# Choosing the 256 best keys by interpolated thresholds, with the small updates on GpSimd and the adaLN sums on VectorE

## The chip, the cores and the metric

The kernel runs on one core of a Trainium2 chip. The metric is the device time of one execution in microseconds. Three runs of the kernel before gave 1230.46, 1232.58 and 1237.68 us, so the median is 1232.58 us.

## The reference

Two decoder layers run one after the other on a sequence of 1024 positions with 1024 features in float32. In each layer:

```
mod = silu(c) @ w_ada + b_ada            # shift, scale, gate: adaLN
h = layer_norm(x) * (1 + scale) + shift
proj = h @ w_in                          # u, v, z_a | q, k, val, z_b | q_idx, k_idx, w_idx
y_a = silu(z_a) * spatial_gating_unit(u, v, ...)         # chunks of 128
score[t, s] = sum_h w_idx[t, h] * relu(q_idx[t, h] . k_idx[s] / 8)   # s <= t only
idx = top_k(score, 256)                  # per row t, 256 keys
y_b = silu(z_b) * softmax(q . k[idx]) @ val[idx]         # 8 heads
x = layer_norm(ALPHA * x + gate * (concat(y_a, y_b) @ w_out))
```

For the work at hand the middle lines matter: every row t has scores for its t + 1 earlier positions, and attention may use only the 256 largest. Rows 0 to 255 have at most 256 keys, so a selection is needed for the six blocks 2 to 7 of 128 rows each, with 384, 512, ..., 1024 columns.

## The kernel before

Rows lie on the 128 partitions. Products with `w_in` and `w_out` are made from high and low float32r halves, three matmuls for each tile of 128 by 512 (L326, L735). A layer goes through these stages:

- The keys, values and half of the indexer queries are projected (`kv`, `queries`). Then `scores` (L496) makes the six score tiles `sc2` to `sc7`: TensorE (L506), a ReLU on ScalarE (L508) and an accumulation on VectorE (L513).
- The remaining projections follow: `v_path`, `queries`, `u_za` and `zb`, one weight pair after the other. The weights are split in two halves by ScalarE and GpSimd (L279, L280). The spatial gating `sgu` (L445) lies between them. Each projection yields after a tile, and after each yield `side()` (L905) takes steps of generators that are not part of the projections. Those are the searches for the thresholds, and, in the second half of the stage, the adaLN sums (`ada_sum`, L166).
- The masks are finished by `select_mask` (L636), `w_out` is loaded and scaled with the adaLN gate (`load_wout`, L710, with products on VectorE and GpSimd at L717 and L720), and the attention runs over the blocks in the order `ORDERS[l]`: 1, 0, 2, 3, ... in the first layer, 4, 5, 6, 2, 3, 7, 1, 0 in the second.

A framework below the kernel gives out buffers and semaphores and settles the order of the instructions on each engine in advance, from a simulated timeline; on the chip each engine then works through its own list in order. All loads go through the one queue of SyncE.

The selection before the change looks for the exact 256th largest score by its bits, one bit per step, and has three forms. Blocks 7, 6 and 5 (`select` with `on_act`, L527) take 31 steps with a sign-and-sum on ScalarE for each block (L544) and two operations on one column on VectorE (L545, L553). Blocks 4 and 3 (`select16`, L590) are searched in two passes of 16 steps over 16-bit keys, with a count (L574) and two operations on one column (L583, L585) for each block. Block 2 takes 31 steps with a count at L519 and L552, L553. `select_mask` then counts twice (L642, L644), numbers the equal scores by a running sum (L647), and makes the mask of 0 and -3e38 with two passes on VectorE (L648, L649) and one on GpSimd (L650).

An adaLN sum adds up eight products of a 128 by 1024 weight tile with one column of the condition. On GpSimd that is a product (L182) and a sum (L184) for each tile. The first layer makes three such sums (its gate and the next layer's shift and scale), 24 tiles; the second layer makes one, 8 tiles. The buffer of a tile is free again for the next load (L163, on the SyncE queue) when its product has been added.

Of the kernel before, what the change touches and what calls it, by code (L numbers as in the profile page):

```python
# [22 lines left out]
S = 1024  # L23
# [4 lines left out]
TOP = 256  # L28
EPS = 1e-5
# [19 lines left out]

class Trunk:  # L50
    BUFS = dict(h=16, ya=4, wr=2, w=6, r=6, kd=2, vv=1, q=2, ga=6, gb=3, gc=4)
    PBUFS = dict(acc=2, s=2, pt=3, o=1)
    GROUPS = ((0, 7, 6, 5), (16, 4, 3), (32, 2))
    MLEAD = 16
# [9 lines left out]
    ADAE = (0, 0, 0)  # L64
# [30 lines left out]
    def consts(self):  # L95
# [9 lines left out]
        nc.gpsimd.memset(self.mhalf, -0.5)  # L105
        self.ones = self.col("ones", 1)
# [389 lines left out]
    def scores(self, l, i):  # L496
        nc = self.nc
        n = (i + 1) * P
        q = self.load_q(l, 1, i)
        sc = self.t(f"sc{i}", [P, n])  # L500
        for h in range(8):
            for c0, w in self.chunks(i):
                self.scn += 1
                pl = self.p(self.SC_PS[self.scn % len(self.SC_PS)])
                for x in range(2):
                    nc.tensor.matmul(pl[:, :w], q[:, h, :], self.KI[x][:, c0:c0 + w], start=(x == 0), stop=(x == 1))  # L506
                r = self.g(self.SC_R[self.scn % len(self.SC_R)])
# [12 lines left out]

    def int_tile(self):
        return self.col("bi", 14, 4, I32)

    def cnt_tile(self):
        return self.col("cnt", 12, 4)

    def select(self, scs, blocks, on_act):  # L527
        nc, G = self.nc, len(blocks)
        ns = [(i + 1) * P for i in blocks]
        cnt = self.cnt_tile()  # L530
        for c in range(G):
            self.count(scs[c], ns[c], 0.0, ALU.is_ge, cnt[:, c:c + 1])
        m = self.int_tile()
        nc.vector.tensor_scalar(m[:, :G], cnt[:, :G], float(TOP), -1.0, op0=ALU.is_lt, op1=ALU.mult)
        f = self.int_tile()
        nc.vector.tensor_scalar(f[:, :G], m[:, :G], 1 << 30, -(1 << 31) if on_act else 0, op0=ALU.bitwise_xor, op1=ALU.bitwise_xor)
        yield
        for b in range(30, -1, -1):
            cnt, dec = self.cnt_tile(), self.int_tile()
            for c in range(G):  # L540
                thr = f[:, c:c + 1].bitcast(F32)
                if on_act:
                    j = self.t("junka", [P, S], I8)
                    nc.scalar.activation(j[:, :ns[c]], scs[c], AF.Sign, bias=thr, accum_out=cnt[:, c:c + 1])  # L544
                    nc.vector.tensor_scalar(dec[:, c:c + 1], cnt[:, c:c + 1], float(2 * TOP - 1 - ns[c]), float(1 << b),  # L545
                                            op0=ALU.is_lt, op1=ALU.mult)
                else:
                    self.count(scs[c], ns[c], thr, ALU.is_ge, cnt[:, c:c + 1])
            f2 = self.int_tile()
            for c in range(G):  # L550
                if not on_act:
                    nc.vector.tensor_scalar(dec[:, c:c + 1], cnt[:, c:c + 1], float(TOP), float(1 << b), op0=ALU.is_lt, op1=ALU.mult)  # L552
                nc.vector.tensor_scalar(f2[:, c:c + 1], dec[:, c:c + 1], f[:, c:c + 1], (1 << b) >> 1,  # L553
                                        op0=ALU.bitwise_xor, op1=ALU.bitwise_xor)
            f = f2
            yield
        if on_act:
            mag, g, up = self.int_tile(), self.int_tile(), self.cnt_tile()
            nc.vector.tensor_scalar(mag[:, :G], f[:, :G], 0x7FFFFFFF, None, op0=ALU.bitwise_and)
            nc.vector.tensor_scalar(up[:, :G], mag[:, :G].bitcast(F32), 1.25 * 2.0 ** -24, 2.0 ** -149, op0=ALU.mult, op1=ALU.max)  # L560
            nc.vector.tensor_tensor(g[:, :G].bitcast(F32), up[:, :G], f[:, :G].bitcast(F32), op=ALU.subtract)
            nc.vector.tensor_scalar(f[:, :G], f[:, :G], -(1 << 31), None, op0=ALU.bitwise_xor)
            cnt, ok = self.cnt_tile(), self.int_tile()
            for c in range(G):
                self.count(scs[c], ns[c], g[:, c:c + 1].bitcast(F32), ALU.is_ge, cnt[:, c:c + 1])
            nc.vector.tensor_scalar(ok[:, :G], cnt[:, :G], float(TOP), None, op0=ALU.is_ge)
            nc.vector.copy_predicated(f[:, :G], ok[:, :G], g[:, :G])
        for c, i in enumerate(blocks):
            self.thr[i] = f[:, c:c + 1].bitcast(F32)
        yield  # L570

    def count16(self, keys, thr, out):
        j = self.t("junkd", [P, 6 * P], BF16)
        self.nc.vector.tensor_scalar(j[:, :keys.shape[1]], keys, thr, None, op0=ALU.is_ge, op1=ALU.add, accum_out=out)  # L574

    def search16(self, keys, t):
        nc, G = self.nc, len(keys)
        for b in range(15, -1, -1):
            cnt, dec, t2 = (self.cnt_tile() for _ in range(3))
            for c in range(G):  # L580
                self.count16(keys[c], t[:, c:c + 1], cnt[:, c:c + 1])
            for c in range(G):
                nc.vector.tensor_scalar(dec[:, c:c + 1], cnt[:, c:c + 1], float(TOP), -float(1 << b), op0=ALU.is_lt, op1=ALU.mult)  # L583
            for c in range(G):
                nc.vector.tensor_scalar(t2[:, c:c + 1], dec[:, c:c + 1], t[:, c:c + 1], float((1 << b) >> 1), op0=ALU.add, op1=ALU.add)  # L585
            t = t2
            yield
        return t

    def select16(self, scs, blocks):  # L590
        nc, G = self.nc, len(blocks)
        store, off, keys = self.u("r", (P, 2 * S), I16), 0, []
        for c, i in enumerate(blocks):
            n = (i + 1) * P
            k = store[:, off:off + n]
            off += n
            hi = scs[c].bitcast(I16).rearrange("p (n two) -> p n two", two=2)[:, :, 1]
            nc.vector.tensor_scalar(k, hi, 0.0, 32767.0, op0=ALU.is_lt, op1=ALU.mult)
            nc.vector.tensor_tensor(k, k, hi, op=ALU.bitwise_xor)
            keys.append(k)  # L600
        t = self.cnt_tile()
        nc.vector.memset(t[:, :G], 0.0)
        yield
        t = yield from self.search16(keys, t)
        neg = self.cnt_tile()
        sg, of = self.cnt_tile(), self.cnt_tile()
        nc.vector.tensor_scalar(neg[:, :G], t[:, :G], 0.0, None, op0=ALU.is_lt)
        nc.vector.tensor_scalar(sg[:, :G], neg[:, :G], -2.0, 1.0, op0=ALU.mult, op1=ALU.add)
        nc.vector.tensor_scalar(of[:, :G], neg[:, :G], 65535.0, None, op0=ALU.mult)
        low = []  # L610
        for c, i in enumerate(blocks):
            n = (i + 1) * P
            lw = self.g("gb", (P, 2 * HALF), U16)[:, :n]
            src = scs[c].bitcast(U16).rearrange("p (n two) -> p n two", two=2)[:, :, 0]
            nc.vector.tensor_scalar(lw, src, sg[:, c:c + 1], of[:, c:c + 1], op0=ALU.mult, op1=ALU.add)
            nc.vector.scalar_tensor_tensor(lw, keys[c], t[:, c:c + 1], lw, op0=ALU.is_equal, op1=ALU.mult)
            k = keys[c].bitcast(U16)
            nc.vector.tensor_scalar(k, keys[c], t[:, c:c + 1], 65535.0, op0=ALU.is_gt, op1=ALU.mult)
            nc.vector.tensor_tensor(k, k, lw, op=ALU.max)
            low.append(k)  # L620
        u = self.cnt_tile()
        nc.vector.memset(u[:, :G], 32768.0)
        yield
        u = yield from self.search16(low, u)
        f, m = self.int_tile(), self.int_tile()
        nc.vector.tensor_copy(f[:, :G], t[:, :G])
        nc.vector.tensor_copy(m[:, :G], u[:, :G])
        f2, m2, f3 = self.int_tile(), self.int_tile(), self.int_tile()
# [431 lines left out]
```

## Time and profile before

| | |
|---|---|
| median of 3 runs | 1232.58 us |
| the profiled execution, its own time | 1233.29 us |
| its span, first to last instruction | 1231.5 us |
| TensorE / VectorE busy | 1119.0 us / 977.5 us |
| ScalarE / GpSimd busy | 707.1 us / 706.5 us |
| mean granted TensorE clock | 0.963 of full speed |

The shares are means over stages that differ. In time, with us from the start of the span: first the adaLN of layer 0 and its first projections to about 110, scores to about 205, projections with the searches to about 410, attention of layer 0 to about 700, scores of layer 1 to about 812, projections with the searches to about 1007, attention to the end. A matmul's busy time includes time in which it waits in the pipeline, so a busy TensorE is not one at its peak.

### The profile page before, as it was taken

The page shows a single profiled execution, that of the slowest core. Times are in us where ns is not written, and L with a number is a line of the kernel's source. Part 1 is how long each engine was busy: PE and PEld are TensorE (multiplying, and loading weights), DVE is VectorE, ACT ScalarE, POOL GpSimd, SP SyncE. Part 2 cuts the span into 40 slices and gives each one's busy share as a digit, 9 for nine tenths or more (in the row PEclk, how much of TensorE's full clock was granted, in tenths as well). Part 3 has the DMA queues.
Part 4 walks back from the last instruction along what each step waited for, and adds up shares of the span by engine and source line. Part 5 has one row for each costly group of instructions (what it writes and reads, how often), then busy time and mean ns, then how long its engine had stood idle before and what let it go on. Part 6 is the DMA issues. An engine that isn't in the chain of part 4 may idle for free.

```text
span 1231.5 us, 18024 instructions
## 1 busy us (share of the span) xinstructions
PE 1119.0 (91%) x5456; PEld 887.3 (72%) x5456; DVE 977.5 (79%) x2776; ACT 707.1 (57%) x1344; POOL 706.5 (57%) x556
## 2 busy tenths in 40 slices
PE   5989999897999499989989999999899967999997
PEld 1568888766788388766667788877678856777885
DVE  6784767998989965788976467599999898878775
ACT  0342655778794164565765345557789535667561
POOL 1574314997794785564765531189633378555753
PEclk9899999998999799999999999999999988999999
DMA  8936332347454474331322463144431434333311
GB/s 257 275 104 165 104 86 79 136 138 222 140 170 154 142 222 125 103 112 44 94 86 69 120 172 86 52 163 137 147 125 52 141 100 142 83 104 86 112 35 60
DMA packets 126777, 152.15 MB, mean 124 GB/s; under 512 B 17108, under 2 KB 94292, under 8 KB 126680
## 3 DMA queue, kind: packets, MB, share of 16 engines
q1 hardware_dynamic: 126680, 151.01, 40.3%
q8 instruction: 43, 0.70, 0.2%
q14 instruction: 54, 0.44, 0.1%
HBM read 111.38 MB, written 35.40 MB: 119 GB/s over the span
## 4 chain that ended last, share of the span: by engine, by line
PE 49%; DVE 30%; issue 7%; ACT 6%; DMA 6%; SPq 2%; POOL 0%; DVEq 0%; ACTq 0%; POOLq 0%
PE pacc L326 18%; PE pacc L735 13%; DVE junkd L574 4%; PE ps L673 4%; PE ppt L693 4%; DVE junkd L519 3%; PE ppt L506 3%; ACT junka L544 3%; PE po L699 2%; PE po L698 2%; PE ps L506 2%; DMA h<-in_w_ada 1%; DVE gb L647 1%; DVE bn L211 1%; DVE bi L553 1%
## 5 line engine op out<-in xcount | busy, mean ns | idle before, releaser
L326 PE MATMUL pacc<-h,w 128*128 128x512 f32 (+2 forms) x2304 | 550.0, 393 | 13.0 <-ACT gc L472 4.8
L326 PEld LDWEIGHTS pacc<-h,w 128*128 128x128 f32 (+1 forms) x2304 | 423.6, 189 | 111.2 <-ACT gc L472 6.4
L280 POOL TENSOR_TENSOR w<-wr,w 128x512 fp32r<-128x512 f32 (+1 forms) x100 | 131.6, 1334 | 168.4 <-ACT w L279 161.2
L544 ACT ACTIVATE junka<-sc,bi 128x1024 int8<-128x1024 f32 x186 | 193.5, 1040 | 51.0 <-DVE bi L553 23.4
L735 PE MATMUL pacc<-h,gc 128*128 128x512 f32 x768 | 196.5, 400 | 2.9 <-ACT gc L279 2.5
L735 PEld LDWEIGHTS pacc<-h,gc 128*128 128x128 f32 x768 | 142.6, 191 | 31.8 <-ACT gc L279 3.2
L513 DVE SCALAR_TENSOR_TENSOR sc<-gc,wi,sc 128x384 f32<-128x384 f32 (+3 forms) x140 | 101.8, 768 | 52.6 <-ACT gc L508 50.1
L673 PE MATMUL ps<-kd,q 128*128 128x512 f32 (+4 forms) x384 | 106.2, 376 | 31.5 <-DVE mx L674 24.8
L697 DVE TENSOR_TENSOR ga<-ppt,ga 128x512 fp32r<-128x512 f32 x144 | 96.6, 684 | 18.1 <-ACT ga L696 17.2
L696 ACT ACTIVATE ga<-ppt 128x512 fp32r<-128x512 f32 x144 | 82.7, 593 | 34.8 <-PE ppt L693 33.6
L574 DVE TENSOR_SCALAR_CACHE_REDUCE junkd<-r,cnt 128x640 bf16<-128x640 int16 (+3 forms) x128 | 102.5, 801 | 0.1
L673 PEld LDWEIGHTS ps<-kd,q 128*128 128x128 f32 x384 | 65.6, 198 | 49.5 <-DVE mx L674 37.1
L682 POOL TENSOR_SCALAR w<-w,rd 128x256 f32<-128x256 f32 (+6 forms) x77 | 62.5, 815 | 42.5 <-DVE rd L681 22.7
L679 ACT ACTIVATE w<-w,mx 128x256 f32<-128x256 f32 (+6 forms) x77 | 60.7, 788 | 42.6 <-DVE mx L674 42.0
L279 ACT ACTIVATE w<-wr 128x512 fp32r<-128x512 f32 (+1 forms) x100 | 56.0, 598 | 44.1 <-DMA wr<-in_w_in 22.0
L693 PE MATMUL ppt<-ident,w 128*128 128x128 f32 x349 | 75.5, 277 | 0.3 <-ACT gc L256 0.3
L216 POOL TENSOR_TENSOR rs<-rs,mhalf 128x1 f32<-128x1 f32 x48 | 32.1, 676 | 73.1 <-DVE rs L215 73.0
L693 PE MATMUL ppt<-ident,ya 128*128 128x128 f32 x227 | 59.1, 277 | 15.4 <-DVE modT L192 15.4
L698 PE MATMUL po<-ga,vv 128*128 128x512 f32 x144 | 62.1, 431 | 9.4 <-DVE gb L705 6.4
L508 ACT ACTIVATE gc<-ppt 128x384 f32<-128x384 f32 (+3 forms) x96 | 47.9, 525 | 36.9 <-PE ppt L506 31.5
L184 POOL TENSOR_TENSOR r<-r,r 128x1024 f32<-128x1024 f32 x28 | 68.2, 2437 | 0.1
L345 POOL TENSOR_TENSOR ga<-ga,ga 128x512 fp32r<-128x512 f32 (+2 forms) x40 | 48.4, 1215 | 33.5 <-ACT ga L344 29.2
(202 smaller groups left out, 2109.4 us busy)
## 6 DMA issues: line engine op xcount, KB each, us to landing
wr<-in_w_in SPq DMA_DIRECT2D x50, 512.0 KB, 4.2
r<-in_w_ada SPq DMA_DIRECT2D x32, 512.0 KB, 4.3
q<-q SPq DMA_DIRECT2D x112, 128.0 KB, 3.0
q<-ga SPq DMA_DIRECT2D x48, 256.0 KB, 2.2
h<-in_w_ada SPq DMA_DIRECT2D x32, 256.0 KB, 5.4
wr<-in_w_out SPq DMA_DIRECT2D x16, 512.0 KB, 4.0
r<-r SPq DMA_DIRECT2D x14, 512.0 KB, 3.4
r<-x SPq DMA_DIRECT2D x12, 512.0 KB, 4.2
```

The lines of the kernel that those rows point to most:

```text
L184: eng.tensor_tensor(acc, acc, w, op=ALU.add)
L280: self.nc.gpsimd.tensor_tensor(lo, src, hi.bitcast(F32), op=ALU.subtract)
L326: self.nc.tensor.matmul(acc[:m, :tn], w[:, k, :m], h[:, k % 2, t0:t0 + tn], start=(k == 0 and i == 0), stop=(k == NK - 1 and i == 2))
L513: nc.vector.scalar_tensor_tensor(sc[:, c0:c0 + w], r[:, :w], wsc, sc[:, c0:c0 + w], op0=ALU.mult, op1=ALU.add)
L544: nc.scalar.activation(j[:, :ns[c]], scs[c], AF.Sign, bias=thr, accum_out=cnt[:, c:c + 1])
L574: self.nc.vector.tensor_scalar(j[:, :keys.shape[1]], keys, thr, None, op0=ALU.is_ge, op1=ALU.add, accum_out=out)
L673: nc.tensor.matmul(ps[:, :w], q[:, g * 4 + h, :], self.KD[x][:, c0:c0 + w], start=(x == 0), stop=(x == 1))
L693: nc.tensor.transpose(pt[:, h * P:(h + 1) * P], pr[h][:, kt * P:(kt + 1) * P], self.ident)
L696: nc.scalar.activation(ph, pt, AF.Copy)
L697: nc.vector.tensor_tensor(pl, pt, ph.bitcast(F32), op=ALU.subtract)
L698: nc.tensor.matmul(o, self.V[:, kt, :], ph, start=(kt == 0), stop=False)
L735: self.nc.tensor.matmul(acc, s[:, k, :], m[:, cs], start=(first and k == i == 0), stop=(not more and k == 3 and i == 2))
```

## The change

All three searches are replaced by one, in two groups: blocks 2, 3, 4 and blocks 5, 6, 7. From the mean and the deviation of the first 256 scores of each row, and from a table that is loaded once (`ztab`), it makes a first threshold and a bracket around it. Then there are six steps. In each, VectorE counts the scores at or above the threshold for the three blocks, and GpSimd narrows the bracket and interpolates the next threshold, all three blocks in one instruction of a few columns. A row has what it needs when the upper end of its bracket counts 248 to 255 scores. The number of rows for which that isn't so is summed by TensorE and read into a register of VectorE. If it isn't 0, a branch runs `exact`, the old bit search, for the three blocks of the group. The masks are made within the same generator: the scores at or above the threshold are set aside by two passes, the up to eight that are still missing are found with `max` (eight largest of a row) and marked with `match_replace`, and a last pass turns the marks into 0 and -3e38. `side()` now takes one step of one group in turn instead of one step of each search. The adaLN sums within the layers run on VectorE, where each tile is one instruction, a product and a sum together (L174, L176).

```
-    GROUPS = ((0, 7, 6, 5), (16, 4, 3), (32, 2))
-    MLEAD = 16
+    GROUPS = ((2, 3, 4), (5, 6, 7))
+    STEPS = 6
-    ADAE = (0, 0, 0)
+    ADAE = (1, 1, 1)
...
     def rope_tables(self):
+        nc.sync.dma_start(self.ztab, a["ztab"][:, 0:36].rearrange("p (k g) -> p k g", k=6))
+        nc.sync.dma_start(self.iota8, a["ztab"][:, 36:44])
...
+    def select(self, masks, blocks, grp):
...
+        for c, i in enumerate(blocks):
+            nc.vector.bn_stats(st[:, 0, :], masks[i][:, 0:256])
+            nc.vector.bn_aggr(mv[:, c, :], st[:, 0:1, :])
...                                  # 9 GpSimd instructions: first threshold V, bracket Z
+        yield
+        for k in range(self.STEPS):
+            for c, i in enumerate(blocks):
+                self.count(masks[i], (i + 1) * P, V[:, 0, c:c + 1], ALU.is_ge, C[:, c:c + 1])
+            pool.tensor_scalar(V[:, 1, :], C, 1.0, -float(MID), op0=ALU.mult, op1=ALU.add)
+            pool.tensor_scalar(M[:, 0, :, :], rep(C, 2), float(TOP), 1.0, op0=ALU.is_lt, op1=ALU.mult)
+            pool.tensor_scalar(M[:, 1, :, :], rep(C, 2), float(TOP), 1.0, op0=ALU.is_ge, op1=ALU.mult)
+            pool.tensor_scalar(M[:, 2, :, :], rep(C, 2), float(TOP), 1.0, op0=ALU.is_lt, op1=ALU.mult)
+            pool.tensor_tensor(pair(Z), pair(Z), M[:, 0:2].rearrange(...), op=ALU.mult)
+            pool.tensor_tensor(pair(U), cols(V)..., M[:, 1:3].rearrange(...), op=ALU.mult)
+            pool.tensor_tensor(Z, Z, U, op=ALU.add)
...                                  # k == 0: 5 more, the first step; k == 5: none
+            elif k + 1 < self.STEPS:
+                pool.tensor_tensor(W[:, 0, :], Z[:, 0, :], Z[:, 2, :], op=ALU.subtract)
+                pool.tensor_scalar(R, Z[:, 3, :], -0.5, 1.0, op0=ALU.min, op1=ALU.mult)
+                pool.tensor_tensor(W[:, 1, :], Z[:, 1, :], R, op=ALU.subtract)
+                pool.tensor_tensor(R, W[:, 1, :], self.minus6[:, :G], op=ALU.pow)
+                pool.tensor_tensor(R, R, W[:, 0, :], op=ALU.mult)
+                pool.tensor_tensor(R, R, Z[:, 1, :], op=ALU.mult)
+                pool.tensor_tensor(V[:, 0, :], Z[:, 0, :], R, op=ALU.subtract)
+            yield
+        pool.tensor_scalar(bad, Z[:, 3, :], float(TOP - 8 - MID), 1.0, op0=ALU.is_lt, op1=ALU.mult)
+        for c in range(G):
+            nc.tensor.matmul(pt[0:1, 0:1], bad[:, c:c + 1], self.ones[:, 0:1], ...)
+        nc.vector.tensor_copy(flag, pt[0:1, 0:1])
+        v = nc.vector.value_load(flag[0:1, 0:1])
+        with self.tc.If(v != 0):
+            for c, i in enumerate(blocks):
+                self.exact(masks[i], (i + 1) * P)       # bit search: 33 counts, then 7 passes
+                nc.vector.memset(Z[:, 2, c:c + 1], 1.5)
+                nc.vector.memset(Z[:, 3, c:c + 1], float(TOP - 8 - MID))
...                                  # 5 GpSimd instructions: Q, how many are missing
+        for c, i in enumerate(blocks):
+            nc.vector.tensor_scalar(w[:, :n], sc, Z[:, 2, c:c + 1], -2.0 * LOW, op0=ALU.is_lt, op1=ALU.mult)
+            nc.vector.scalar_tensor_tensor(sc, w[:, :n], LOW, sc, op0=ALU.add, op1=ALU.min)
+            yield
+            nc.vector.max(m8, sc)
+            nc.vector.tensor_tensor(m8, m8, Q[:, c, :], op=ALU.min)
+            yield
+            nc.vector.match_replace(sc, m8, sc, LOW)
+            nc.vector.tensor_scalar(sc, sc, LOW, NEG, op0=ALU.not_equal, op1=ALU.mult)
+            yield
-    def select_mask(self, sc, i):
...
             while owed >= 1:
                 owed -= 1
-                for g in gens:
-                    next(g, None)
+                while gens and next(gens[0], 0) == 0:
+                    gens.pop(0)
+                gens.append(gens.pop(0)) if gens else None
```

## Rows read from the trace of the kernel before

**Rows 1.** The page's first part: busy time of each engine

```profile
PE 1119.0 (91%) x5456; PEld 887.3 (72%) x5456; DVE 977.5 (79%) x2776; ACT 707.1 (57%) x1344; POOL 706.5 (57%) x556
```

**Rows 2.** Windows: stretch, length; busy PE, PEld, DVE, ACT, POOL; PEclk, DMA, GB/s

```profile
205.00:435.00 230.00, 196.95 (x966) 158.00 (x965) 214.61 (x776) 151.08 (x273) 185.74 (x126) 0.93 0.51 161
812.00:1050.00 238.00, 210.02 (x1013) 166.80 (x1011) 224.44 (x811) 161.16 (x284) 150.40 (x102) 0.94 0.40 129
...
410.00:435.00 25.00, 8.14 (x43) 6.55 (x42) 22.55 (x34) 8.54 (x18) 18.27 (x9) 0.59 0.46 152
...
990.00:1050.00 60.00, 41.34 (x184) 32.94 (x182) 55.38 (x99) 26.11 (x42) 49.25 (x26) 0.83 0.41 137
...
435.00:700.00 265.00, 244.98 (x1230) 193.00 (x1231) 191.35 (x486) 150.56 (x296) 167.28 (x148) 0.98 0.36 107
```

**Rows 3.** Waits of PE, 205 to 435 and 812 to 1050: us, times, longest

```profile
PE ppt L693 <- DVE modT L192: 15.4, 1, 15.4
...
PE ps L673 <- DVE mx L674: 15.3, 5, 9.3
```

**Rows 4.** Groups of VectorE instructions, 205 to 435: sum us, mean ns, idle before

```profile
L574 DVE TENSOR_SCALAR_CACHE_REDUCE junkd<-r,cnt 128x640 bf16<-128x640 int16 (+1 forms) x64 | 51.2, 801 | 0.0
...
L553 DVE TENSOR_SCALAR bi<-bi,bi 128x1 int32<-128x1 int32 x124 | 23.2, 204 | 0.4
...
L647 DVE TENSOR_TENSOR_SCAN gb<-gb 128x384 f16<-128x384 f16 (+5 forms) x6 | 9.7, 1622 | 0.0
L649 DVE SCALAR_TENSOR_TENSOR sc<-sc,bi,gb 128x384 f32<-128x384 f32 (+5 forms) x6 | 9.4, 1559 | 0.0
L457 DVE SCALAR_TENSOR_TENSOR ya<-po,vg,bsum 128x128 f32<-128x128 f32 x32 | 9.2, 334 | 0.0
...
L644 DVE TENSOR_SCALAR_CACHE_REDUCE gb<-sc,bi 128x384 f16<-128x384 f32 (+5 forms) x6 | 5.6, 930 | 0.0
...
L514 DVE TENSOR_TENSOR sc<-sc,mask 128x128 f32<-128x128 f32 x1 | 0.3, 279 | 0.0
...
L622 DVE MEMSET cnt<- 128x2 f32 x1 | 0.1, 60 | 0.0
```

**Rows 5.** Groups of VectorE by shape, whole run, like passes elsewhere

```profile
L855 DVE SCALAR_TENSOR_TENSOR ga<-h,cond,ga 128x512 f32<-128x512 f32 x14 | 12.2, 874 | 0.1
...
L720 DVE TENSOR_TENSOR h<-wr,h 128x1024 fp32r<-128x1024 f32 x4 | 5.6, 1412 | 0.2 <-ACT h L719 0.2
...
L220 DVE TENSOR_SCALAR q<-q,mv,rs 128x1024 f32<-128x1024 f32 x6 | 4.8, 808 | 1.4 <-POOL rs L216 1.4
```

**Rows 6.** Groups of GpSimd, 205 to 435

```profile
L184 POOL TENSOR_TENSOR r<-r,r 128x1024 f32<-128x1024 f32 x21 | 51.0, 2430 | 0.1
...
L182 POOL TENSOR_SCALAR r<-r,cond 128x1024 f32<-128x1024 f32 x24 | 30.1, 1257 | 26.0 <-PE ps L506 17.4 <-DMA r<-in_w_ada 8.6
...
L650 POOL TENSOR_SCALAR sc<-sc 128x384 f32<-128x384 f32 (+5 forms) x6 | 9.8, 1628 | 15.8 <-DVE bi L630 11.8 <-DVE sc L649 4.0
```

**Rows 7.** GpSimd by shape, whole run: the smallest ones, and L682 at two sizes

```profile
L216 POOL TENSOR_TENSOR rs<-rs,mhalf 128x1 f32<-128x1 f32 x48 | 32.1, 676 | 73.1 <-DVE rs L215 73.0
...
L682 POOL TENSOR_SCALAR w<-w,rd 128x1024 f32<-128x1024 f32 x10 | 11.6, 1155 | 1.6 <-DVE rd L681 1.2 <-DVE nmb L229 0.3
...
L682 POOL TENSOR_SCALAR w<-w,rd 128x256 f32<-128x256 f32 x19 | 10.1, 539 | 3.9 <-DVE rd L681 3.9
...
L107 POOL MEMSET ones<- 128x1 f32 x1 | 0.1, 99 | 0.0
```

**Rows 8.** ScalarE, whole run: the sign-and-sum of the old search

```profile
L544 ACT ACTIVATE junka<-sc,bi 128x1024 int8<-128x1024 f32 x186 | 193.5, 1040 | 51.0 <-DVE bi L553 23.4 <-DVE bi L545 13.7 <-DVE bi L536 6.6
```

**Rows 9.** SyncE queue: a wait in all, an issue (start, us); a load (KB, us to landing)

```profile
SPq L163 <- POOL r L184: 42.4, 17, 5.3
...
7.15 0.43 SPq L126 DMA_DIRECT2D invf<-in_inv_freq  x1
...
r<-cs_tab SPq DMA_DIRECT2D x16, 128.0 KB, 7.2
```

More of the change, by code (lines that the diff above doesn't have):

```diff
@@ L22 @@
 D = 1024
-S = 1024
+S = SEQ = 1024
 DEPTH = 2
@@ L28 @@
 TOP = 256
+MID = 252
+LOW = -2.0 ** 126
 EPS = 1e-5
@@ L47, in two_pi_parts, with start_table @@
     return parts
+def start_table():
+    import numpy as np
+    from statistics import NormalDist
+    nd = NormalDist()
+    tab = np.zeros((P, 6, 6), np.float32)
+    for i in range(2, NB):
+        for p in range(P):
+            n = i * P + p + 1
+            z = nd.inv_cdf(1.0 - (MID + 0.5) / (n + 1))
+            above = lambda y: n * (1.0 - nd.cdf(y)) - MID
+            tab[p, :, i - 2] = (z - 2.0, z, z + 2.0, min(above(z + 2.0), -9.0), above(z - 2.0), 1.0 / (n * nd.pdf(z)))
+    return np.concatenate([tab.reshape(P, 36), np.tile(np.arange(8, dtype=np.float32), (P, 1))], axis=1)
 class Trunk:
@@ L105, in consts @@
         nc.gpsimd.memset(self.mhalf, -0.5)
+        self.half6 = self.col("half6", 1, 6)
+        nc.gpsimd.memset(self.half6, 0.5)
+        self.minus6 = self.col("minus6", 1, 6)
+        nc.gpsimd.memset(self.minus6, -1.0)
+        self.iota8 = self.col("iota8", 1, 8)
+        self.ztab = self.t("ztab", [P, 6, 6])
         self.ones = self.col("ones", 1)
@@ L494, with scores @@
     SC_R = ('gc',)
-    def scores(self, l, i):
+    def scores(self, l, i, sc):
         nc = self.nc
@@ L499, in scores @@
         q = self.load_q(l, 1, i)
-        sc = self.t(f"sc{i}", [P, n])
         for h in range(8):
@@ L521, in int_tile @@
     def int_tile(self):
-        return self.col("bi", 14, 4, I32)
+        return self.col("bi", 8, 1, I32)
     def cnt_tile(self):
[L525 to L530, printed above, removed]
-        for c in range(G):
[L532 to L536, printed above, removed]
-        yield
-        for b in range(30, -1, -1):
[L539 to L554, printed above, removed]
-            f = f2
[L556 to L628, printed above, removed]
-        nc.vector.scalar_tensor_tensor(f2[:, :G], f[:, :G], 16, m[:, :G], op0=ALU.logical_shift_left, op1=ALU.bitwise_or)
-        nc.vector.tensor_scalar(m2[:, :G], f2[:, :G], 31, 0x7FFFFFFF, op0=ALU.arith_shift_right, op1=ALU.bitwise_and)
-        nc.vector.tensor_tensor(f3[:, :G], f2[:, :G], m2[:, :G], op=ALU.bitwise_xor)
-        for c, i in enumerate(blocks):
-            self.thr[i] = f3[:, c:c + 1].bitcast(F32)
-        yield
@@ L636, in select_mask @@
[L636 to L650 removed]
+        return self.col("cnt", 8, 1)
@@ L925, in layer @@
                 for i in range(2, NB):
-                    masks[i] = self.scores(l, i)
-                gens = []
-                for kind, *grp in self.GROUPS:
-                    scs = [masks[i] for i in grp]
-                    gens.append(self.select16(scs, grp) if kind == 16 else self.select(scs, grp, kind == 0))
+                    masks[i] = self.t(f"sc{i}", [P, (i + 1) * P])
+                    self.drain(self.scores(l, i, masks[i]))
+                gens += [self.select(masks, b, k) for k, b in enumerate(self.GROUPS)]
                 self.sgu_setup(l)
@@ L947, in layer @@
         for t in range(-1, T + 2):
-            for i in order:
-                if i > 1 and t == max(2 * order.index(i) - self.MLEAD, -1):
-                    self.select_mask(masks[i], i)
             for _ in range(self.WB.count(t)):
@@ L1049 @@
     f = (np.float64(10000.0) ** (-np.arange(0, 64, 2) / 64.0)).astype(np.float32)
-    inputs = dict(inputs, inv_freq=np.tile(f, 4).reshape(P, 1))
-    for name in _INS + ["inv_freq"]:
+    inputs = dict(inputs, inv_freq=np.tile(f, 4).reshape(P, 1), ztab=start_table())
+    for name in _INS + ["inv_freq", "ztab"]:
         arr = np.ascontiguousarray(inputs[name])
```

83 lines of the change are left out of this document (67 added, 16 removed).

## The prediction

> **What bounds the kernel now.** I read the busy times first [rows 1]: TensorE is busy for 91% of the span, so no change can win more than its gaps. Next I asked the windows where the gaps lie, stage by stage. In each layer one stretch stands out, the projections with the searches and the turn to attention [rows 2]: 205 to 435 in layer 0, with TensorE busy for 196.95 of 230 us, and 812 to 1050 in layer 1, with 210.02 of 238. That is 33 + 28 = 61 us of idle TensorE, and VectorE is busy for 214.61 and 224.44 us there, 93 and 94%. It is the bound of these stretches: its groups show next to no idle time before them [rows 4]. The worst of it is the turn itself. From 410 to 435 TensorE works 8.14 of 25 us at a mean granted clock of 0.59, and from 990 to 1050 it works 41.34 of 60 at 0.83 [rows 2]. The waits say for what [rows 3]: 15.4 us for a four-column sum (L192) and 15.3 us for the attention's row minimum (L674). Both are short VectorE instructions that stand in its list behind the passes of the masks. In the attention after it, from 435 to 700, TensorE is busy for 244.98 of 265 us [rows 2], 92.4%.
>
> So the most that can come back is the 61 us and what the low clock cost: at full speed the work of the two turns would take 8.14 x 0.59 = 4.8 and 41.34 x 0.83 = 34.3 us, 10 us less. The ceiling is 71 us.
>
> **What goes.** In layer 0 the searches and masks are 656 VectorE instructions in 39 groups, from L574 with 51.2 us to L622 with 0.1 [rows 4]. These instructions overlap their neighbours, so I count from the other side: what stays is 19 groups with 59 us in all, from L457 with 9.2 to L514 with 0.3 [rows 4]; at least 214.6 - 59 = 156 us of VectorE go. Layer 1 has the same search, so 224.4 - 156 = 68 us stay there. ScalarE loses 186 sign passes, 193.5 us in both layers [rows 8]. GpSimd loses the adaLN products and sums, 51.0 + 30.1 = 81 us in layer 0 and, with 8 tiles instead of 24, 27 in layer 1, and 9.8 us of masks in each [rows 6].
>
> **What VectorE gets, per layer.** A count over all six blocks cost 5.6 us at L644 [rows 4]; with six readouts at about 0.1 that is 6.1, and six steps make 37. The statistics of 256 columns can't cost more than a count each: 5 us at most. The masks need five passes over 384 to 1024 columns, 4224 for the six blocks. Two have one input: 808 ns for 1024 columns at L220 [rows 5], so 3.3 us each. One has two inputs, like L649 with 9.4 us [rows 4], which was often held up. `max` and `match_replace` appear nowhere in the trace; I bound them by a count, 5.6, and the running sum at L647, 9.7 [rows 4], and take 5.6 for each, since they read one float32 row like a count. Six small ones of 0.2, as L553 [rows 4], are added: 28 us, with 20 and 42 as the ends. The flags take 2. An adaLN tile becomes one two-input instruction on 1024 columns: 1412 ns as L720, or twice L855's 874, or no less than L220's 808 [rows 5]. I take 1.41, for the same shape: 34 us in layer 0 (ends 19 and 42), 11 in layer 1.
>
> The sums are 59 + 37 + 5 + 28 + 34 + 2 = 165 us in layer 0 and 68 + 37 + 5 + 28 + 11 + 2 = 151 in layer 1, instead of 215 and 224. At about 204 and 214 us for the stretches (below) VectorE is busy for 81 and 71%, so it stops being the bound; at the upper ends layer 0 has 187, which would still fit, barely.
>
> **What GpSimd gets.** By the diff a group issues 9 instructions for the start, 12 + 4 x 14 + 7 in the steps and 6 after them: 90, so 180 in a layer, all of at most 24 columns. The nearest rows are L682 with 1155 ns for 1024 columns and 539 for 256 [rows 7]; a straight line through both leaves 0.33 us for no columns. The ends are the memset of one column with 99 ns and the power at L216 with 676 [rows 7]. Five of the 90 are powers. I take 0.35 and 0.68: 85 x 0.35 + 5 x 0.68 = 33 us per group, 66 per layer (ends 18 and 122). GpSimd's load becomes 185.7 - 81 - 9.8 + 66 = 161 us in layer 0, and 150.4 - 27 - 9.8 + 66 = 180 in layer 1. It is now as full as VectorE, and that is the thing to watch: the high and low halves of the next weights (L280) stand in the same list, behind updates that wait for counts.
>
> **Is the search done in time?** A step is three counts, some 3 us, and 14 updates, 5.2 us; the other group's counts run during them. GpSimd has half its time for the 66 us, so both groups end some 130 us after the scores, and the masks 28 us later: near 365 in layer 0, where the projections now end near 410. In the lists all steps are there too: the stage has 44 yields, at 1.1 steps each 48, and two groups need 38. The passes that held up the turn now lie inside the projections, so the waits of [rows 3] go. What is late next there is `w_out`: its load, the product with the gate and the split on GpSimd.
>
> **The branch** has no row. Two groups in two layers jump over some 420 VectorE instructions each (three blocks, 33 counts and 31 x 2 small operations). If the jump has to bring in its target from memory, the nearest row is the slowest load, 7.2 us [rows 9]; if not, it costs near 0. So it is 0 to 29 us of VectorE in all, and while it stands, everything behind it in VectorE's list waits: the products of the projections and so, with two accumulators, TensorE. I take 1 us of visible time each, 4 in all, because VectorE now has slack. A gain isn't in it. [...]
>
> **Smaller things.** Two loads on SyncE's queue at the start push the first weights back by two issues of 0.43 us [rows 9]: 0.9 us. The adaLN loads keep their number; their queue waited 42.4 us for L184 to free a buffer [rows 9], and behind them stand the weights. A tile is now freed after 1.4 instead of 3.7 us of work, so I count nothing; if VectorE lags, this cover is gone.
>
> **The sum.** At full clock TensorE needs 197 - 3 = 194 us in layer 0 and 210 - 7 = 203 in layer 1. With one of twenty us idle, between none in the scores and the 7.6% of the attention, that is 204 and 214: 26 + 24 = 50 us less. Less 4 for the branches and 1 for the start, the profiled execution's 1233.3 becomes 1188; it lay 0.7 above the median, so the forecast is 1187 us.
>
> **Rivals.**
> 1. All idle time comes back: 1233 - 71 = 1162. For it: three engines are relieved at once. Against it: VectorE and GpSimd stay 70 to 85% busy, and the attention with a like mix loses 7.6%.
> 2. The stage runs like the attention, 92.4%: 210 and 220 us, a gain of 38; and the four jumps show in part or whole, up to 29. Between 1233 - 38 + 1 = 1196 and 1224, middle 1212.
> 3. GpSimd becomes the bound. If an update costs what the power costs, 0.68, its load is 95 + 122 = 217 us in layer 0 and 114 + 122 = 236 in layer 1; at VectorE's old 93% these take 233 and 253 us, 18 more than before: 1251. It wins nothing from 0.63 us an update on. For it: no row shows an update of this shape but the power. Against it: the line through L682.
> 4. The branch is taken, so the change doesn't do what it says. All 384 rows of a group must get a count of 248 to 255 within six counts. The interpolation stays in a bracket, and once a row is in, it stays in; but one row with many equal scores or a bent distribution is enough. Then a group pays 3 x 32 x (0.93 + 2 x 0.2) = 128 us of VectorE at L644 and L553 [rows 4] and 10 for the passes, of which the 40 us that VectorE has idle hide some: one group in one layer gives 1187 + 98 = 1285, more groups more.
>
> **Chances.** Forecast, with a range of its own from 1170 to 1205: 0.55. Rival 1: 0.10. Rival 2: 0.13. Rival 3: 0.12, of which 0.07 lies near no change and 0.05 slower. Rival 4: 0.10, slower. Within 0.5%, 6 us, this kernel can't be told from no change. So faster is 0.78, the same 0.07, slower 0.15. The range for 8 in 10 goes from 1160 to 1240: it takes in rivals 1 and 2 and most of 3, and leaves out the taken branch and the worst GpSimd case.
>
> **What would show it.** Right: per layer 36 counts of 0.6 to 1.3 us and no sign pass on ScalarE; VectorE near 165 and 151 us in the two stretches; no wait of 15 us at the turn, and its clock near 1; GpSimd's updates near 0.35 us. Wrong: instructions of `exact` on VectorE; updates above 0.6 us; TensorE waiting for weights split by GpSimd; gaps of several us on VectorE at the four flags; or masks that end after the projections.

## The result, and the profile after

The changed kernel takes 1307.05 us, the median of 4 runs (1305.79 to 1309.25), against 1231.91 us for the kernel before beside it (1230.46 to 1237.68, 4 runs). The ratio is 1.060, with a 95% interval from 1.057 to 1.064: slower by 6%, where the forecast was 1187 us. Its profiled execution has a span of 1307.5 us.

The page's first part answers to [rows 1] (busy time, share of the span, instructions):

```profile
PE 1135.2 (87%) x5480; PEld 899.3 (69%) x5480; DVE 815.8 (62%) x1744; ACT 501.9 (38%) x972; POOL 679.7 (52%) x846
```

Every engine but TensorE has less to do: VectorE by 162 us, ScalarE by 205, GpSimd by 27. TensorE has 16 us more to do, and its share fell from 91 to 87%. So no engine has become too full; TensorE waits. The windows of the changed kernel show where (the columns of [rows 2]; first two stretches of layer 0 and the one after them, then the like stretch of layer 1 and the one after it):

```profile
222.00:288.00 66.00, 56.99 (x328) 44.86 (x326) 56.14 (x98) 14.07 (x25) 60.77 (x89) 0.95 0.63 201
288.00:355.00 67.00, 24.35 (x113) 18.67 (x114) 48.80 (x102) 1.15 (x2) 37.15 (x110) 0.62 0.27 87
355.00:435.00 80.00, 80.00 (x348) 66.06 (x349) 11.62 (x26) 15.61 (x26) 25.91 (x21) 0.98 0.29 84
...
925.00:985.00 60.00, 20.21 (x87) 14.00 (x88) 39.80 (x89) 2.43 (x3) 25.54 (x90) 0.59 0.20 60
985.00:1022.00 37.00, 37.00 (x161) 30.57 (x160) 6.97 (x14) 5.62 (x10) 12.71 (x10) 0.98 0.26 78
```

The turns that were slow before are gone: TensorE's longest wait for the row minimum was 9.3 us and is 2.2. A new hole is there earlier: from 288 to 355 TensorE is busy for 24 of 67 us at a mean granted clock of 0.62, and 43 us are lost; from 925 to 985 it is 20 of 60 at 0.59, and 40 us. Behind each hole TensorE works without a gap, and the other engines have next to nothing to do. TensorE's longest waits, in the form of [rows 3] but over the whole run (us in all, times, longest):

```profile
PE ppt L606 <- POOL sb L603: 39.7, 2, 23.3
PE po L443 <- DVE gc L244: 22.8, 3, 9.8
PE pacc L350 <- DVE ya L493: 18.1, 5, 6.3
```

The longest waiter is L606, the matmul that sums the flag of a group, that is, the number of its rows for which the search has failed. TensorE's timeline in layer 0 shows what stands behind it (start, length, what, how many; in brackets the idle time before it and its releaser):

```profile
284.95 1.09 PE L443 MATMUL po<-q,gc 128*64 128x128 f32 x16
291.06 8.59 PE L350 MATMUL pacc<-h,w 128*128 128x512 f32 x24 [5.01 <-DVE ya L493]
322.96 0.29 PE L606 MATMUL ppt<-ones,sb 128*1 128x1 f32 x6 [23.30 <-POOL sb L603]
323.18 1.11 PE L475 MATMUL ppt<-ident,ya 128*128 128x128 f32 x4
331.04 1.98 PE L443 MATMUL po<-q,gc 128*64 128x128 f32 x16 [6.74 <-DVE gc L244]
332.95 0.29 PE L606 MATMUL ppt<-ones,sb 128*1 128x1 f32 x6
333.17 1.12 PE L475 MATMUL ppt<-ident,ya 128*128 128x128 f32 x4
```

L475 and L443 are the transposes and the matmuls of the gating unit (`sgu`), which runs over eight row blocks. Six are done by 286 us. The last two stand behind the two flag matmuls in TensorE's list, and a flag can't be summed before its group's six rounds of counts and updates are over. The projections of `u` are evacuated from their accumulators by a product with the gating unit's output (L493). There are two accumulators for all projections, so the stage can't go on before the last two blocks are done. One tiny matmul thus makes the whole stage wait for the end of the search; the runs below test this reading. What the search does in that time is one chain across two engines (VectorE, then GpSimd, of the same kernel):

```profile
308.14 0.61 DVE L544 TENSOR_SCALAR_CACHE_REDUCE junkd<-sc,sv 128x384 int8<-128x384 f32 x1 [1.66 <-POOL sv L600]
...
313.59 1.01 DVE L544 TENSOR_SCALAR_CACHE_REDUCE junkd<-sc,sv 128x768 int8<-128x768 f32 x1 [3.11 <-POOL sv L600]
...
322.60 1.01 DVE L544 TENSOR_SCALAR_CACHE_REDUCE junkd<-sc,sv 128x768 int8<-128x768 f32 x1 [3.02 <-POOL sv L600]
```

```profile
317.21 0.20 POOL L579 TENSOR_SCALAR sv<-sc 128x3 f32<-128x3 f32 x1 [1.23 <-DVE junkd L544]
...
322.64 0.26 POOL L603 TENSOR_SCALAR sb<-ss 128x3 f32<-128x3 f32 x1
```

### The profile page after: what moved, and what is told of

The parts are those of the page before. It is cut to its first block, busy times and chain, and to the rows that moved or that the text cites. A ratio compares the mean times of both kernels' runs of the same rounds, so it can differ in the third digit from the quotient of the medians.

```text
span 1307.5 us, 16769 instructions
## 1 busy us (share of the span) xinstructions
PE 1135.2 (87%) x5480; PEld 899.3 (69%) x5480; DVE 815.8 (62%) x1744; ACT 501.9 (38%) x972; POOL 679.7 (52%) x846
## 5 line engine op out<-in xcount | busy, mean ns | idle before, releaser
L350 PEld LDWEIGHTS pacc<-h,w 128*128 128x128 f32 (+1 forms) x2304 | 428.5, 191 | 121.1 <-DVE ya L493 19.9
L536 DVE SCALAR_TENSOR_TENSOR sc<-gc,wi,sc 128x384 f32<-128x384 f32 (+3 forms) x140 | 104.9, 791 | 29.3 <-ACT gc L531 27.0
L544 DVE TENSOR_SCALAR_CACHE_REDUCE junkd<-sc,sv 128x384 int8<-128x384 f32 (+2 forms) x72 | 67.7, 940 | 34.6 <-POOL sv L600 29.4
L727 DVE TENSOR_TENSOR wr<-wr,r 128x1024 f32<-128x1024 f32 x8 | 14.6, 1829 | 116.2 <-DMA wr<-in_w_out 116.2
L708 PE MATMUL po<-ga,vv 128*128 128x512 f32 x144 | 62.3, 432 | 8.7 <-DVE gb L715 7.1
L369 POOL TENSOR_TENSOR ga<-ga,ga 128x512 fp32r<-128x512 f32 (+2 forms) x40 | 53.8, 1350 | 26.0 <-ACT ga L368 20.0
L709 PE MATMUL po<-ga,vv 128*128 128x512 f32 x144 | 63.2, 439 | 3.1 <-DVE ga L707 3.0
L200 DVE SCALAR_TENSOR_TENSOR r<-r,cond,r 128x1024 f32<-128x1024 f32 x28 | 42.9, 1531 | 33.8 <-DMA r<-in_w_ada 33.6
L496 ACT ACTIVATE gc<-pacc 128x512 f32<-128x512 f32 x16 | 9.4, 589 | 139.7 <-PE pacc L350 139.7
```

The source lines that it names most:

```text
L350: self.nc.tensor.matmul(acc[:m, :tn], w[:, k, :m], h[:, k % 2, t0:t0 + tn], start=(k == 0 and i == 0), stop=(k == NK - 1 and i == 2))
L708: nc.tensor.matmul(o, self.V[:, kt, :], ph, start=(kt == 0), stop=False)
L709: nc.tensor.matmul(o, self.V[:, kt, :], pl, start=False, stop=(kt == i))
```

## The experiments

A tag is a set of buffers that the framework gives out in turn, here in PSUM, where the results of this kernel's matmuls stand. The theory after the result (A): the flag's tile comes from the tag `pt`, which the gating unit's transposes use too, with three buffers handed out in the program's order. The flag is written between the unit's steps, so the steps behind it wait for its end. The rivals: the branch cuts the engines' lists in two (B); the lists were laid out for a branch body of 31 steps (C); the adaLN sums on VectorE (D); the rounds themselves are too long (E). Ratios are to the kernel before, run on the same chip, with 95% intervals.

**Flag and branch left out.**

```diff
-        pt = self.p("pt")
-        for c in range(G):
-            nc.tensor.matmul(pt[0:1, 0:1], bad[:, c:c + 1], ...)
 ...
-        v = nc.vector.value_load(flag[0:1, 0:1])
-        with self.tc.If(v != 0):
 ...
```

> The flag matmul, its copy, the loaded value and the branch with the bit search are left out in both layers (the fallback is missing; these inputs don't take it). Theory A (the flag takes a buffer of the PSUM tag pt in program order, so the last two steps of the gating unit and everything behind them wait for the end of the search): 1200 us (1180 to 1225), TensorE busy again between 288 and 355 us. Theory B (the branch parts the lists of the engines): 1200. Theory C (the list was settled with the branch's 31-step body in the planned time): 1200. Theory D (the adaLN passes on VectorE and the gate write that blocks SyncE's queue): 1290 or more. Theory E (the search's 6 rounds between VectorE and GpSimd are simply too long for the work beside them): 1280 or more.

Measured: 1222.0 us (1220.4 to 1228.2), ratio 0.989 (0.983 to 0.994). The hole is gone (TensorE is busy for 57.9 us of 288 to 355), so D and E fall as its cause, and the adaLN part alone is not what made the kernel slow. The time lies inside A's range, but 22 us above the one figure that A, B and C share.

**The branch with an empty body.**

```diff
             for c, i in enumerate(blocks):
-                self.exact(masks[i], (i + 1) * P)
                 nc.vector.memset(Z[:, 2, c:c + 1], 1.5)
```

> Flag, loaded value and branch stay, but the branch's body holds only the six memsets, no bit search (the fallback would be wrong if it were taken; it is not). Theory A: 1305 us, no change. Theory B: 1305. Theory C (planned length of the body): 1200. Theory D and E: 1300.

Measured: 1303.6 us (1296.0 to 1307.3), ratio 1.052 (1.046 to 1.058). C falls: without its bit search the body is a few memsets, and the time stays.

**The flag without the branch.**

```diff
         nc.vector.tensor_copy(flag, pt[0:1, 0:1])
         yield
-        v = nc.vector.value_load(flag[0:1, 0:1])
-        with self.tc.If(v != 0):
 ...
```

> The flag matmul and its copy stay where they are, the loaded value and the branch go. Theory A: 1290 us (1280 to 1303), only the four stalls of 2.5 us at the branches go. Theory B: 1200. Theory C: 1200. Theory D and E: 1290 to 1300.

Measured: 1304.0 us (1299.6 to 1306.6), ratio 1.055 (1.049 to 1.060). B falls: with no branch in the program the kernel is as slow. A said 1290, and the time is 1 us above the upper end of its range. Its interval overlaps those of the changed kernel and of the empty body, so not even the 10 us of stalls at the four branches, which A expected back, can be told from nothing.

**The flag in another PSUM tag.** One word changes; flag, branch and bit search stay.

```diff
         pool.tensor_scalar(bad, Z[:, 3, :], ...)
-        pt = self.p("pt")
+        pt = self.p("s")
```

> One word is changed: the flag's PSUM tile comes from the tag s (two buffers, between the scores and the attention) instead of pt, which the gating unit's transposes use. Flag, branch and bit search all stay. Theory A: 1205 us (1185 to 1230), and the last gating step's matmul ends before 300 us instead of 349. Theory B, C, D and E: 1300 to 1310.

Measured: 1226.8 us (1219.9 to 1229.4), ratio 0.990 (0.984 to 0.995): with this word the kernel beats the one before by 1%. As without the flag, that is 22 us above A's figure, and within its range. The order of TensorE's list in layer 0, cut to lines and counts, says why (first with the tag `pt`, then with `s`). L224 and L214 are matmuls of the adaLN sums, L612 is the branch. The profile counts each matmul of L443, L606, L224 and L214 twice, so 3 here are 6 there:

```
L443x8 L350x24 L443x8 L350x24 L606x3 L475x4 L612x1 L443x8 L606x3 L475x4 L224x2 L612x1 L214x12 L443x8 L214x4 L350x120
L443x8 L350x24 L214x2 L443x8 L214x6 L350x24 L443x8 L214x8 L443x8 L350x66 L606x3 L350x20 L612x1 L350x18 L606x3 L350x20
```

In the second list all transposes of the gating unit (L475) are ahead of this piece, its last products (L443) come before the first flag, and 66 projection matmuls stand between. The timeline of that kernel:

```profile
302.87 1.09 PE L443 MATMUL po<-q,gc 128*64 128x128 f32 x16
310.79 17.82 PE L350 MATMUL pacc<-h,w 128*128 128x512 f32 x66 [6.82 <-DVE ya L493]
328.54 0.29 PE L606 MATMUL ps<-ones,sb 128*1 128x1 f32 x6
328.76 8.93 PE L350 MATMUL pacc<-h,w 128*128 128x512 f32 x38
338.58 0.29 PE L606 MATMUL ps<-ones,sb 128*1 128x1 f32 x6 [0.89 <-POOL sb L603]
```

The gating unit ends near 304 instead of 349 us; A had said before 300. The searches end no earlier than in the changed kernel (flags at 328 and 338, there at 323 and 333), but now TensorE has work while they run, and the flags of both layers cost it 0.9 us of waiting instead of 39.7. Its windows:

```profile
288.00:355.00 67.00, 54.48 (x261) 43.92 (x261) 44.48 (x94) 6.78 (x12) 49.05 (x121) 0.87 0.40 129
...
925.00:985.00 60.00, 58.81 (x265) 48.29 (x264) 24.95 (x47) 8.48 (x16) 24.08 (x27) 1.00 0.21 67
```

**The flag later, in the old tag.**

```diff
+        for _ in range(4):
+            yield
         bad = small("sb", 1)[:, 0, :]
```

> The flag's tile stays in the tag pt, but each group's flag, branch and masks come four program steps later, behind the last step of the gating unit. Theory A (it is the place in the program's order that counts, through the rotation of the three pt buffers): 1227 us (1215 to 1237), as with the flag in s. If the flag must not share the tag at all, wherever it stands: 1290 to 1310.

Measured: 1228.8 us (1224.4 to 1230.5), ratio 0.992 (0.989 to 0.995). The tag alone is harmless; the tag together with a place ahead of the gating unit's last steps is not. That is what A says, and the time is within 2 us of its figure. That the rotation of the three buffers makes that order is read from these two edits and the lists, and not shown by itself; no run had `pt` with more buffers.

**The adaLN part undone.**

```diff
-    ADAE = (1, 1, 1)
+    ADAE = (0, 0, 0)
```

> The changed kernel with the adaLN sums back on GpSimd, as before; search, flag in the tag pt and branch stay. Theory A (the flag's place): the last steps of the gating unit still wait for the flag: 1305 us (1290 to 1325). Theory D (adaLN on VectorE is at fault): 1235 us or less.

Measured: 1350.6 us (1349.0 to 1352.0), ratio 1.092 (1.090 to 1.094): D falls once more. But the loss is 26 us above the upper end of A, too. The waits of TensorE say why:

```profile
PE ppt L606 <- POOL sb L603: 79.7, 2, 65.2
```

With the sums on GpSimd (1.3 to 2.4 us each in [rows 6]) the search's small updates stand behind them, the rounds take longer, and the flag comes later still, at 362 instead of 323 us in layer 0: one wait of 65 us instead of 23. While TensorE waits for the flag, each round's length is paid in full: that wait is 40 us longer (79.7 against 39.7), and by the ratios, 1.092 against 1.060, the kernel is some 39 us slower.

**The adaLN part alone, on the kernel before.**

```diff
-    ADAE = (0, 0, 0)
+    ADAE = (1, 1, 1)
```

> The kernel before with one change: the adaLN sums on VectorE. VectorE was busy 93% of 205 to 435 us there; some 24 passes of 1.5 us in layer 0 and 8 in layer 1 come on top, while GpSimd loses 55 us. If VectorE was the bound of that stretch, as the prediction read it: 1255 us (1242 to 1275). If TensorE's order was the bound and VectorE's full list only followed it: 1228 to 1238, no change.

Measured: 1270.6 us (1267.0 to 1273.7), ratio 1.028 (1.025 to 1.030). In the old kernel VectorE was the bound, as the prediction read it: 32 passes more cost 34 us, 16 above the figure and within the range. VectorE is busy for 92% of 205 to 470, where it was 93% of 205 to 435 [rows 2], and over the whole run TensorE waits 32.7 us for the row minimum, where it was 24.8 (the last line is the kernel before):

```profile
205.00:470.00 265.00, 224.57 (x1060) 178.50 (x1058) 244.34 (x831) 164.34 (x299) 126.78 (x94) 0.91 0.50 156
```

```profile
PE ps L673 <- DVE mx L674: 32.7, 22, 6.7
```

```profile
PE ps L673 <- DVE mx L674: 24.8, 23, 9.3
```

**Flag in `s`, adaLN on GpSimd** (both edits above).

> The flag in the tag s, and the adaLN sums back on GpSimd. If the adaLN passes on VectorE (35 us in the middle of layer 0) are what the repaired kernel still lacks of the forecast: 1195 to 1210 us. If GpSimd's list then stretches the search's rounds (its 14 small updates stand behind adaLN passes of 1.3 us): 1230 to 1245. If neither: 1222 to 1230, since TensorE's own 1120 us of work bound it.

Measured: 1231.7 us (1226.6 to 1236.0, 10 runs), ratio 0.996 (0.994 to 0.998). If anything that is worse than with the sums on VectorE, by 5 us or 0.6%. Moving the same 32 passes to VectorE cost 34 us beside the old search and nothing beside the new one. It doesn't follow that the passes are free there, for the time falls in the expectation's second case: the search's updates stand behind the sums on GpSimd, and the first flag of layer 0 comes at 401 instead of 328 us:

```profile
400.81 0.29 PE L606 MATMUL ps<-ones,sb 128*1 128x1 f32 x6
```

Now TensorE has other work while it comes. No run takes the passes off VectorE without this.

**No selection at all** (search, flag, branch and masks left out; the attention adds the raw scores). Theory F: TensorE's own work and order bound the rest. Theory G: the rounds and masks still hold the repaired kernel.

```diff
     def select(self, masks, blocks, grp):
-        nc, G, pool = ...
 ...
+        for _ in range(2):
+            yield
```

> The whole selection is left out in both layers: no search, no flag, no branch, no masks; the attention adds the raw scores instead (so the output is not the reference's). It shows the floor that any faster top-k can reach in this kernel. Theory F (TensorE's own order and work, some 1120 us busy, bound the rest; the forecast of 1187 us counted as recoverable idle time what is no idle time of the selection's): 1210 to 1222 us, under 15 us below the kernel with the flag in s. Theory G (the search's rounds and masks on VectorE still hold the repaired kernel): 1175 to 1195.

Measured: 1197.6 us (1194.6 to 1201.6), ratio 0.969 (0.964 to 0.974). This is the floor for this order of the other work, and it lies between the two theories: a search that is free wins 3.1%, some 39 us, over the kernel before, and the kernel with the repaired flag has a third of that. G was nearer: what is left of the search costs about 2%. In its windows TensorE has in the middle of layer 0 what the kernel with `s` lacks there, 65.6 instead of 54.5 of 67 us:

```profile
288.00:355.00 67.00, 65.61 (x324) 54.88 (x325) 15.87 (x33) 11.70 (x19) 20.07 (x16) 0.97 0.50 153
```

**The updates on VectorE**, the powers still on GpSimd, with the flag in `s`; then the same with the adaLN sums on GpSimd. E stands here for the crossings between the two engines.

```diff
-            pool.tensor_scalar(V[:, 1, :], C, 1.0, -float(MID), ...)
+            nc.vector.tensor_scalar(V[:, 1, :], C, 1.0, -float(MID), ...)
 ...
-        pt = self.p("pt")
+        pt = self.p("s")
```

> Flag in the tag s; the search's small updates on VectorE instead of GpSimd, only the two powers stay on GpSimd. Some 180 more VectorE instructions of 0.14 to 0.2 us per layer, 30 us, but only one crossing to GpSimd and back in each round. Theory E (the rounds' crossings between the two engines hold up the gating unit's chain on VectorE and GpSimd): 1205 to 1218 us. Theory F: 1222 to 1230, no change. If VectorE's own load counts: 1235 or more.

> As the one before, and the adaLN sums on GpSimd: neither engine's list holds what the other one waits for round by round. Theory E: 1205 to 1215 us, the best of these. Theory F: 1220 to 1230.

Measured: 1244.3 us (1240.9 to 1246.5, 10 runs), ratio 1.006 (1.003 to 1.008), and 1269.2 us (1262.2 to 1272.6), ratio 1.025 (1.019 to 1.031). E falls in this form too: with fewer crossings between the engines the first is slower than the kernel with `s`, not faster, by 17 us or 1.6%, as the third case had it. TensorE waits there 11.3 us for the gating unit's products on VectorE (L481), where it waited 1.1; for the evacuations (L493) it waits no longer than before, 14.3 us against 17.8. The second was to be the best and is 25 us worse than the first. The same small instructions take longer on VectorE on average when GpSimd has the adaLN sums (L581 in the first kernel, then in the second):

```profile
L581 DVE TENSOR_SCALAR sm<-sc 128x6 f32<-128x6 f32 x24 | 6.0, 252 | 0.0
```

```profile
L581 DVE TENSOR_SCALAR sm<-sc 128x6 f32<-128x6 f32 x24 | 14.0, 583 | 0.0
```

The average hides two kinds. In the second kernel 17 of the 24 take 0.15 to 0.19 us as usual, and 7 take 1.3 to 2.4, each held beside a GpSimd pass over 512 or 1024 columns until that ends (both engines; the last line is a usual one):

```profile
272.11 2.44 DVE L581 TENSOR_SCALAR sm<-sc 128x6 f32<-128x6 f32 x1
272.13 2.39 POOL L208 TENSOR_TENSOR r<-r,r 128x1024 f32<-128x1024 f32 x1
...
293.11 0.16 DVE L581 TENSOR_SCALAR sm<-sc 128x6 f32<-128x6 f32 x1
```

In all VectorE is busy for 28 us more there (894.2 against 866.6), in spite of 28 adaLN passes and 4 first products less. It happens the other way round, too. In the changed kernel 11 of the 340 small updates on GpSimd, powers aside, took over 1 us: 9 of them ran beside an adaLN pass of VectorE (L200) and 2 beside a mask pass (L627). Of the 110 that ran beside counts alone only powers took over 0.3 us (the others 0.28 at most). One of the 9, and the same instruction beside a count:

```profile
294.36 1.27 DVE L200 SCALAR_TENSOR_TENSOR r<-r,cond,r 128x1024 f32<-128x1024 f32 x1
294.42 1.28 POOL L583 TENSOR_TENSOR ss<-ss,sm 128x12 f32<-128x12 f32 x1
...
304.89 0.21 POOL L583 TENSOR_TENSOR ss<-ss,sm 128x12 f32<-128x12 f32 x1
```

How much of the 25 us comes from this no run shows.

**Flag in `s`, adaLN shared out.**

```diff
-    ADAE = (1, 1, 1)
+    ADAE = (0, 1, 1)
```

> The flag in the tag s; the gate's adaLN sums (8 passes in each layer) on GpSimd, the next layer's shift and scale (16 passes in layer 0) on VectorE. With all of them on VectorE it was 1227 us and with all on GpSimd 1232, where the selection's floor was 1198. If the two engines' loads are what is left to share out: 1215 to 1222 us. If it is the search's own chain or TensorE's order: 1225 to 1235, no change.

Measured: 1236.5 us (1230.2 to 1239.8, 12 runs), ratio 0.998 (0.996 to 1.001): no different from the kernel before, 1% worse than with all sums on VectorE, and 1.5 us above the range for "no change". So none of the three places of the sums wins what is left.

## Why the prediction was wrong

The forecast stood at 1187 us, 0.963 of the kernel before. From there to 1.060 there are 9.7%, some 120 us, and the runs part them: from the forecast to the floor without any selection, 0.969, some 7 us; from the floor to the kernel with the flag in `s`, 0.990, some 26 us; from there to the changed kernel, some 87 us. The last is the step that failed.

**The flag.** The step that failed is the price of the flags: "The flags take 2", as VectorE's work. They cost TensorE 39.7 us of waiting and the kernel some 87. That a flag is also three matmuls in TensorE's list, that they wait for the last link of the search's chain, and that they take a tile of a tag which the gating unit needs, it did not see. Its question was put to the wrong place: "Is the search done in time?" was asked for the attention. For that its "near 365" came true, with the flags at 323 and 333 us and the masks done at 363 (the first and the last pass of the masks):

```profile
337.71 1.37 DVE L626 TENSOR_SCALAR gb<-sc,ss 128x384 bf16<-128x384 f32 x3 [2.69 <-DVEq L612]
...
362.19 1.08 DVE L634 TENSOR_SCALAR sc<-sc 128x640 f32<-128x640 f32 x2
```

The first one who needed the search's end was the gating unit, which can be done by 304, as the kernel with `s` shows. The sentence "In the lists all steps are there too" counted the steps of the program and not what each step lets through: the two groups' flags, the 15th and 16th steps, fall among the gating unit's last ones.

**Five per cent idle.** The terms 204 and 214 us for the stretches, with one of twenty us idle, gave 50 us. With the whole selection gone TensorE still has gaps, and the gain is 39 us. So even a free search brings back less than the term, and the idle time that VectorE's old passes caused was smaller than the 61 us that the prediction put down to them.

**Rest of the search.** Of the 26 us between the floor and the kernel with `s` a part has its place. TensorE waits 17.8 us there for the evacuations of L493, a wait that the floor's kernel doesn't have. They stand in VectorE's list behind counts, and a count waits for GpSimd's update: it is the flag's mistake again, in small. At the end of the gating unit (VectorE of the kernel with `s`; TensorE's side is the line at 310.79 above):

```profile
305.04 1.01 DVE L544 TENSOR_SCALAR_CACHE_REDUCE junkd<-sc,sv 128x768 int8<-128x768 f32 x1 [2.14 <-POOL sv L600]
...
308.48 1.12 DVE L481 SCALAR_TENSOR_TENSOR ya<-po,vg,bsum 128x128 f32<-128x128 f32 x4
...
310.05 1.28 DVE L493 TENSOR_TENSOR ya<-ya,pacc 128x512 f32<-128x512 f32 x2
```

Moving the updates or the adaLN sums did not win the 26 us; which edit would is open.

**What was right.** VectorE was the bound before, as the adaLN part alone shows. The body of the branch did not run: no instruction of `exact` is in the trace. The sizes held too. The groups of VectorE in the changed kernel (us in all, mean ns), by the prediction 74 for the counts with their readouts (which took 5.9 beside the row below), 40 for 28 adaLN tiles of 1.41, and 11.2 and 11.2, for both layers:

```profile
L544 DVE TENSOR_SCALAR_CACHE_REDUCE junkd<-sc,sv 128x384 int8<-128x384 f32 (+2 forms) x72 | 67.7, 940 | 34.6 <-POOL sv L600 29.4 <-POOL sv L574 4.0
L200 DVE SCALAR_TENSOR_TENSOR r<-r,cond,r 128x1024 f32<-128x1024 f32 x28 | 42.9, 1531 | 33.8 <-DMA r<-in_w_ada 33.6
L630 DVE MAX8 m<-sc 128x8 f32<-128x384 f32 (+5 forms) x12 | 10.5, 878 | 0.0
L633 DVE MATCH_REPLACE8 sc<-m,sc 128x384 f32<-128x384 f32 (+5 forms) x12 | 10.4, 872 | 0.0
```

GpSimd's updates were put at 0.35 us and the powers at 0.68. In the rounds the updates took 0.19 to 0.37 us on average and the power 0.88; with the start and the end it was 114 us for both layers, where 132 were taken, so rival 3 (GpSimd the bound) fell:

```profile
L597 POOL TENSOR_TENSOR sr<-sw,minus 128x3 f32<-128x3 f32 x16 | 14.0, 876 | 0.7
L579 POOL TENSOR_SCALAR sv<-sc 128x3 f32<-128x3 f32 x24 | 8.8, 367 | 20.2 <-DVE junkd L544 15.1 <-DVE mv L237 3.8
...
L600 POOL TENSOR_TENSOR sv<-ss,sr 128x3 f32<-128x3 f32 x16 | 3.1, 194 | 0.5
```

**Rival 2, the jumps.** All four branches show a gap on VectorE, between the 0 and the 7.2 us of the prediction's bounds (waits of the changed kernel, on VectorE and on GpSimd):

```profile
DVE gb L626 <- DVEq L612: 5.4, 2, 2.7
DVE rs L239 <- DVEq L612: 4.6, 2, 2.5
```

```profile
POOL sk L618 <- DVEq L612: 14.0, 4, 5.7
```

That is 10 us of VectorE, 2.5 each, where 1 of visible time was taken. The run with the empty body shows that the gap goes with the body that is passed over: there the jumps pass over six memsets instead of some 420 instructions, and VectorE's gaps come to 0.4 us in all:

```profile
DVE gb L625 <- DVEq L612: 0.4, 2, 0.2
```

What fills the 2.1 to 2.7 us of a gap no view shows. In time the gaps can't be told from nothing. Without the branch the slow kernel stayed slow, and without flag and branch the ratio is 0.989, next to 0.990 with both of them and the tag `s`. So the 4 us of the sum are not refuted.

**Slips that change nothing.** The middle of rival 2, between 1196 and 1224, is 1210 and not 1212. The mask pass of GpSimd (L650) took 12.0 us in layer 1 of the kernel before, not the 9.8 of layer 0 that the prediction used for both.

## What to carry to other kernels

When a change adds a small instruction to an engine that works in order, ask three things of it: which chain it waits for, what stands behind it in that engine's list, and whose buffers it takes in the program's order; its own duration, 0.3 us here, does not say what it costs. A check that is needed late should be written late, or on buffers that nobody else turns over: here one word decided between 6% slower and 1% faster. And before hoping for the idle time of a stage, leave the suspected work out and time that floor: here it was 3.1%, and the forecast was below it.

## What the runs showed of the hardware

- `max` (8 values) and `match_replace` over 384 to 1024 columns cost 0.88 and 0.87 us on average, hardly less than a count of like length (0.94).
- In the rounds of the changed kernel an operation of GpSimd on 3 to 12 columns took 0.19 to 0.37 us on average; a power of 3 columns took 0.88, one of a single column 0.68 [rows 7].
- In the changed kernel a branch of VectorE that jumps over a body of some 420 instructions left a gap of 2.1 to 2.7 us on that engine. Over six memsets the gap was 0.2 us.
- VectorE and GpSimd held each other up here and there: with the updates on VectorE and the adaLN sums on GpSimd a VectorE operation on 6 columns (L581), 0.15 to 0.19 us in 17 of 24 cases, took up to 2.44 us beside a GpSimd sum of 1024 columns. In the changed kernel 9 of 340 GpSimd updates took 1.0 to 1.3 us beside VectorE's adaLN passes. Beside VectorE's counts alone none but powers took more than 0.28.
- From 288 to 355 us of the changed kernel, with TensorE idle for 43 of 67 us, its mean granted clock was 0.62, and a transpose of the gating unit (L475) took 435 ns on average. From 222 to 288 us, at a clock of 0.95, it took 281.
